# K partial sums seeded into PSUM, adaLN spans of 1024 columns and a token-major gate/up in one decoder block on one Trainium2 core

## The chip, the cores and the metric

The kernel runs on one NeuronCore of a Trainium2 chip. The core has five engines with a program each: TensorE (PE, matmuls into the accumulators in PSUM), VectorE (DVE), ScalarE (ACT), GpSimd (POOL) and SyncE (SP, which here issues nearly all DMA transfers). They wait for each other through semaphores, and each runs its own instructions in order. The metric is the device time of one execution in microseconds (us), taken as the median of the runs shown.

## What is computed

One decoder layer on 256 tokens with 2048 channels, in fp32. All projections are written as three matmuls in a rounded fp32 format: each operand is split into a high part and the rest, and high x high, high x rest and rest x high are summed in PSUM. Cut to what matters:

```python
mod = silu(c) @ ada_w + ada_b                    # 2048 x 12288
sh1, sc1, g1, sh2, sc2, g2 = split(mod, 6)       # adaLN, 2048 columns each
h = rms_norm(x, mix_pre_g) * (1 + sc1) + sh1
q, k, v, a, g = split(h @ w_in)                  # 2048 x 5120, 1024 columns each
attn = moba_attention(q, k, v)                   # 8 heads, 256 tokens are one key block: causal attention
u = causal_depthwise_conv(a * sigmoid(g), conv_w, conv_b)   # 1024 channels, 31 taps
u = silu(layer_norm(u, conv_ln_g, conv_ln_b))
x = x + g1 * rms_norm(concat(attn, u) @ w_out, mix_post_g)  # 2048 x 2048
h = rms_norm(x, ffn_pre_g) * (1 + sc2) + sh2
y = (silu(h @ w_gate) * (h @ w_up)) @ w_down     # 2048 x 5632 twice, 5632 x 2048
out = x + g2 * rms_norm(y, ffn_post_g)
```

## The kernel before

**Tiles.** The 256 tokens are two tiles of 128 (t = 0, 1; NT in the code). The K dimension is cut into blocks of 128 rows, output columns into groups of 512. A weight load brings up to four K blocks of one group, 1 MB, into one of five raw buffers (`weights`, L595; L619 and L636 are variants for short segments). ACT copies the high part of two K blocks into `wh` (L610), DVE subtracts it for the rest `wl` (L611), and TensorE multiplies.

**Jobs.** A `Job` (L289) is one output group over one segment of K. It holds two of the four PSUM tiles `pa`, one for each t. `multiply_all` (L656) cuts it into units of one or two K blocks and one t. There are two forms. In `mm` (L677) the tokens are the stationary operand and 512 weight columns move: three matmuls for a K block, the result lies token-major. In `side` (L668) 128 weight columns are stationary and all 256 tokens move: six matmuls of 256 columns for a K block and t (t then names one half of the output columns), and the result lies channel-major, as the next stage wants it. Before, `side` is used for all of w_in but v, and for gate and up; `mm` for v, w_out and w_down.

**Partial sums.** Where K is cut into segments, `put` (L709) stores the first segment's result from PSUM to SBUF on ACT (L715) and adds each later one to it on DVE (L717). The last segment is added in the same way; what follows (sigmoid and product for a and g, silu and product for gate and up, the square for the norm of y, L954) then reads SBUF. In w_in the cuts come from `cuts`: four segments for a and g (groups 6 to 9), three for groups 0, 2, 4 and four for groups 1, 3, 5 (the q, k, v columns). w_out has two segments, w_down three (`parts`), gate and up of the first four FFN groups four each (`fcuts`); the other seven FFN groups run over all of K.

**adaLN.** `ada` (L453) makes one span of 512 (or, in early chunks, 256) columns of one of the six vectors from loads of 1 MB (96 in all). Each load is summed on PE (L476: the vector c, padded to 32 columns, against the load; four K blocks in four strips of the array at once) or on DVE (L485, L487: multiply by a column of c and add to a tile `t2`). The letter in `mode` decides: p is PE, d is DVE, a is open: the planner gives each load to PE, but leaves it to DVE when DVE has nothing queued. `sums` (L518) then sums over the partitions for shift and scale columns, L512 spreads the gate rows g1 and g2 over all partitions, and L514 multiplies them into `gain`. There are three tiles in the `t2` pool; adaLN sums, attention, the chunks of h and the gate products share them.

**Stages.** `chunks` cuts K of w_in: for each chunk the spans of SC1 and SH1 are made, then that chunk of h (`h_chunk`, L534), then the w_in segments that end there. When all of a and g is there, `conv` (L759) runs: `nact` of eight channel tiles are multiplied by the taps on ACT (L788) and added on DVE (L791), the others run on DVE alone (L774). `layer_norm` (L804) and then the second K half of w_out wait for it. `attention` (L873) runs in between. Then come y1's norm, x1, `h2_chunk` (L1113), gate and up (`gate_evac` L978, `up_evac` L994), w_down in three parts, and the last norm with the output stores (L1186, L1187).

**Order.** The program is written by a planner (`Plan.order`, L154). It simulates the engines with a cost for each task and emits the tasks in the order in which they start there, so each engine's order is fixed at build time. On each engine the ready task with the smallest `pri` goes first; matmul units of the projections have 3.0, evacuations 0.0. DMA loads come from two queues, weights and adaLN. An adaLN load goes ahead of the weights from weight index `before`, may use a gap from index `after`, and otherwise weights go first while fewer than `nw` are open. For G1 these are `g1_before` and `g1_from`, for SC2 and SH2 `c_before` and `c_after`.

Of the kernel before, what the change touches and what calls it, by code (L numbers as in the profile page):

```python
# [16 lines left out]
P = 128  # L17
D = 2048
# [25 lines left out]
 'g1_before': 23,  # L44
 'c_before': (-192, -5, 77, 198),
 'first': 0,
 'pri': {'conv': 10.889,
         'att': 1.269,
         'g1': 2.484,
         's2': 2.504,  # L50
         'g2': 8.462,
         'cap': 1.455,
         'ln': 2.276,
         'glu': 6.517,
         'h': 0.32,
         'turn': 7.06,
         'hid': 8.565,
         'h2': 2.033},
 'silu': 1,
 'h1': 'DADDDADA',  # L60
 'h2': 'DADDAAAA',
# [4 lines left out]
 'nact': 6,  # L66
 'stagger': 4,
 'stagger1': 4,
 'joint': 2,
# [7 lines left out]
 'g1_from': 51,  # L77
 'c_after': (50, 119, -180, -13),
 'g2_from': 0}
# [209 lines left out]
class Job:  # L289
# [11 lines left out]
def block_kernel(ctx, tc, x, c, ada_w, ada_b, mix_pre_g, mix_post_g, w_in, conv_w, conv_b,  # L301
# [16 lines left out]
    hd_pool = ac_pool = t2_pool  # L318
    if CFG["uni"] < 2:
        hd_pool = Slots([sbt([P, 512], "hd%d" % i) for i in range(CFG["heads"])])  # L320
    if CFG["uni"] < 1:
        ac_pool = Slots([sbt([P, 512], "ac%d" % i) for i in range(CFG["acc"])])
    pri = CFG["pri"]
    br_pool = Slots([sbt([1, 512], "brow")])
# [14 lines left out]
        "w0": ("Q0", [P, 2, 2, 512], F32R), "w1": ("Q1", [P, 2, 2, 512], F32R), "w2": ("Q2", [P, 2, 2, 512], F32R),  # L339
        "conv": ("CV", [P, CT * (256 + HALO) + CT * 256], F32), "x1": ("CV", [P, NT, D], F32),  # L340
# [44 lines left out]
    nc.vector.memset(mhalf, -0.5)  # L385
    cpad = sbt([P, KB, 32], "cpad")
# [835 lines left out]
```

## Time and profile before

| what | value |
|---|---|
| median of 3 runs | 1223.05 us (1222.06 to 1223.63) |
| the profiled execution's own time | 1223.58 us |
| its span, first to last instruction | 1221.8 us |
| mean granted TensorE clock | 0.993 |
| DMA | 307.71 MB, mean 252 GB/s |
| adaLN loads | 96 of 1 MB, median 7.4 us from issue to landing |
| POOL busy | 16.2 us |

In a row of the profile, PE is TensorE's matmuls and PEld its weight loads, which overlap them. L717 is line 717 of the kernel before. The records of a matmul are longer than the distance between two of them, since they are pipelined: the pace is read from the starts, not from the lengths. In the page's slices each digit is the busy share of a fortieth of the span in tenths.

### The profile page before, as it was taken

The numbers are of one execution on the slowest core, as the hardware profiler recorded it, in microseconds if no ns is written. First come the engines' busy times: TensorE is split into PE (matmuls) and PEld (weight loads), VectorE is DVE, ScalarE is ACT, GpSimd is POOL, SyncE is SP. The second block draws the span as 40 slices with busy tenths as digits, with TensorE's granted clock in tenths as the row PEclk, the third lists the DMA queues.
The fourth block names the chain that finished last, engine by engine and source line by source line (L and its number), as shares of the span: only waits on it lengthen the run. The fifth ranks groups of instructions, "written<-read, shape, count | busy, mean of one in ns | idle before, by whom it ended". The sixth has DMA issues, their size and how long they took to land.

```text
span 1221.8 us, 19898 instructions
## 1 busy us (share of the span) xinstructions
PE 1196.4 (98%) x8275; PEld 1072.2 (88%) x8275; DVE 877.6 (72%) x1121; ACT 599.7 (49%) x860; POOL 16.2 (1%) x29
## 2 busy tenths in 40 slices
PE   5999999999999989999999999999999999999997
PEld 4899799997558769999998789999988999999886
DVE  4799889999978789998788996444555455455554
ACT  3643344998965465534454344434433444444441
POOL 1000000000000010000000000000000000000000
PEclk9999999999998999999999999999999999999999
DMA  9999996558997989988558997655556555555532
GB/s 334 343 341 340 370 348 207 177 179 302 343 383 253 326 315 375 323 297 274 173 185 324 365 363 254 196 174 179 198 175 192 187 173 184 195 173 179 200 104 69
DMA packets 160507, 307.71 MB, mean 252 GB/s; under 512 B 5244, under 2 KB 21920, under 8 KB 159648
## 3 DMA queue, kind: packets, MB, share of 16 engines
q1 hardware_dynamic: 159520, 304.11, 72.5%
q0 software_dynamic: 544, 2.11, 0.5%
q8 instruction: 65, 1.06, 0.4%
q10 hardware_dynamic: 352, 0.21, 0.1%
q14 instruction: 26, 0.21, 0.0%
HBM read 304.32 MB, written 2.10 MB: 251 GB/s over the span
## 4 chain that ended last, share of the span: by engine, by line
PE 89%; ACT 4%; DMA 3%; DVE 1%; issue 1%; SPq 1%; POOL 0%; POOLq 0%; DVEq 0%; ACTq 0%
PE pa L674 54%; PE pa L680 10%; PE pa L682 10%; PE pa L681 10%; PE pt L476 3%; DMA raw<-in_ada_w_dram 2%; ACT prod L788 2%; ACT wh L610 1%; PE pt L518 1%; DMA xt<-in_x_dram 1%; DVE t L487 1%; PE pt L512 1%; SPq L626 0%; DVE wl L611 0%; PE pt L825 0%
## 5 line engine op out<-in xcount | busy, mean ns | idle before, releaser
L674 PE MATMUL pa<-h,wh 128*128 128x256 f32 x3840 | 701.6, 284 | 0.0
L611 DVE TENSOR_TENSOR wl<-raw,wh 128x1024 fp32r<-128x1024 f32 x372 | 451.3, 1223 | 271.8 <-ACT wh L610 270.8
L610 ACT ACTIVATE wh<-raw 128x1024 fp32r<-128x1024 f32 x372 | 392.6, 1060 | 498.0 <-PE pa L674 291.1
L674 PEld LDWEIGHTS pa<-h,wh 128*128 128x128 f32 x3840 | 593.9, 188 | 6.4 <-issue 2.7
L674 PE MATMUL pa<-h,wl 128*128 128x256 f32 x1920 | 540.9, 282 | 0.0
L674 PEld LDWEIGHTS pa<-h,wl 128*128 128x128 f32 x1920 | 363.9, 190 | 0.5 <-issue 0.2
L487 DVE SCALAR_TENSOR_TENSOR t<-raw,cact,t 128x512 f32<-128x512 f32 (+1 forms) x238 | 160.9, 676 | 7.6 <-DVE stats L832 0.3
L680 PE MATMUL pa<-wh,hid 128*128 128x512 f32 x352 | 140.9, 400 | 0.0
L682 PE MATMUL pa<-wh,hid 128*128 128x512 f32 x352 | 139.6, 397 | 0.0
L681 PE MATMUL pa<-wl,hid 128*128 128x512 f32 x352 | 139.6, 397 | 0.0
L681 PEld LDWEIGHTS pa<-wl,hid 128*128 128x128 f32 x352 | 66.4, 189 | 16.5 <-issue 0.7
L680 PEld LDWEIGHTS pa<-wh,hid 128*128 128x128 f32 x352 | 66.4, 189 | 16.5 <-issue 0.7
L682 PEld LDWEIGHTS pa<-wh,hid 128*128 128x128 f32 x352 | 66.4, 189 | 16.1
L788 ACT ACTIVATE prod<-conv,taps 128x256 f32<-128x256 f32 x180 | 74.9, 504 | 0.2 <-DVE conv L791 0.2
L791 DVE TENSOR_TENSOR conv<-conv,prod 128x1536 f32<-128x1536 f32 x30 | 52.6, 1753 | 2.1 <-ACT prod L788 1.9
L476 PE MATMUL pt<-raw,cpad 128*32 128x512 f32 (+1 forms) x384 | 45.7, 571 | 5.5 <-DMA raw<-in_ada_w_dram 5.4
L476 PEld LDWEIGHTS pt<-raw,cpad 128*32 128x32 f32 x384 | 9.1, 114 | 21.7 <-issue 10.0
L680 PE MATMUL pa<-wh,mixa 128*128 128x512 f32 x64 | 28.0, 438 | 0.0
L680 PE MATMUL pa<-wh,h 128*128 128x512 f32 x64 | 26.9, 421 | 0.0
L682 PE MATMUL pa<-wh,mixa 128*128 128x512 f32 x64 | 26.3, 412 | 0.0
L681 PE MATMUL pa<-wl,mixa 128*128 128x512 f32 x64 | 26.3, 410 | 0.0
L774 DVE SCALAR_TENSOR_TENSOR conv<-conv,taps 128x256 f32<-128x256 f32 x60 | 25.7, 480 | 0.0
(154 smaller groups left out, 786.5 us busy)
## 6 DMA issues: line engine op xcount, KB each, us to landing
raw<-in_ada_w_dram SPq DMA_DIRECT2D x96, 1024.0 KB, 7.4
raw<-in_w_gate_dram SPq DMA_DIRECT2D x44, 1024.0 KB, 5.3
raw<-in_w_up_dram SPq DMA_DIRECT2D x44, 1024.0 KB, 5.2
raw<-in_w_down_dram SPq DMA_DIRECT2D x44, 1024.0 KB, 5.1
raw<-in_w_in_dram SPq DMA_DIRECT2D x32, 1024.0 KB, 6.8
raw<-in_w_out_dram SPq DMA_DIRECT2D x16, 1024.0 KB, 7.9
raw<-in_w_in_dram SPq DMA_DIRECT2D x16, 512.0 KB, 7.4
xt<-in_x_dram SPq DMA_DIRECT2D x2, 1024.0 KB, 10.1
```

The source lines that it names most:

```text
L476: nc.tensor.matmul(ps.t[32 * (k % 4):32 * (k % 4) + 32, 0:wd], cpad[:, k0 + k, :], view()[:, k, :], start=me == mine[0] and k < 4, stop=me ...
L487: nc.vector.scalar_tensor_tensor(acc.t[:, 0:wd], view()[:, k, :], s, acc.t[:, 0:wd], op0=ALU.mult, op1=ALU.add)
L512: a = add("PE", 0.86, min(prio, pri["cap"]), lambda: nc.tensor.matmul(pt.t, ones, acc.t, start=True, stop=True), [a], [pt, acc])
L610: a = add("ACT", 0.475 * m, p, lambda raw=raw, u=u, m=m, wh=wh: nc.scalar.activation(wh.t[:, 0:m, :], raw.t[:, u:u + m, :], AF.Copy), [loa ...
L611: b = add("DVE", 0.567 * m, p, lambda raw=raw, u=u, m=m, wh=wh, wl=wl: nc.vector.tensor_sub(wl.t[:, 0:m, :], raw.t[:, u:u + m, :], f32(wh. ...
L674: nc.tensor.matmul(job.ps[t].t[:, 256 * n:256 * n + 256], w.t[:, j, cs], h, start=u == 0 and j == r and n == 0 and i == 0, stop=end and j ...
L680: nc.tensor.matmul(job.ps[t].t, hi, wh.t[:, j, :], start=u == 0 and j == r, stop=False)
L681: nc.tensor.matmul(job.ps[t].t, hi, wl.t[:, j, :], start=False, stop=False)
L682: nc.tensor.matmul(job.ps[t].t, lo, wh.t[:, j, :], start=False, stop=end and j == r + len(ks) - 1)
L774: nc.vector.scalar_tensor_tensor(cacc[:, k, :], upad[:, k, i:i + 256], w, cacc[:, k, :], op0=ALU.mult, op1=ALU.add)
L788: nc.scalar.activation(T("prod")[:, i % 2, k, :], upad[:, k, i:i + 256], AF.Copy, scale=w)
L791: pa = add("DVE", 0.267 * CFG["nact"] + 0.07, pri["conv"] + 0.001 * i, lambda i=i: nc.vector.tensor_add(cacc[:, nv:], cacc[:, nv:], T("pro ...
```

## The change

1. **Seeds (`inj`).** A job whose group has an earlier segment gets a `base`: before its first matmul ACT copies the stored partial sum from SBUF into the job's PSUM tile, and all its matmuls accumulate onto it. The copy waits for the earlier segment's store and until the job before it has issued its first unit. The result of every segment but the last is copied out on ACT; the last one is read from PSUM where it is used. The DVE adds of `put` are gone.
2. **adaLN spans.** `ada` takes any span of K columns; of 1024 columns it keeps two sums (two tiles, or on PE two rows of strips in one PSUM tile). G1 and SC2/SH2 are cut 512, 512, 1024, G2 1024, 1024; the chunks of w_in lose the cut at 6. The modes change: in loads, 28 p, 20 a and 48 d become 12 p, 48 a and 36 d.
3. **Token-major gate/up.** Gate and up use `mm`. The product of silu(gate) and up lies token-major, is turned by four PE transposes for each group and t, and is split into high part and rest from PSUM.
4. **Order.** New priorities, cuts, loading order of adaLN, conv channels on ACT (`nact` 6 to 5), and split of the tiles at the ends of w_out and w_down (`stagger`, `stagger1`, `joint`). In `side` the two matmuls with `wh` now follow each other. The output stores alternate between SP's and ACT's queues.

The core of the diff:

```diff
- 'g1_before': 23,
- 'c_before': (-192, -5, 77, 198),
+ 'g1_before': 68,
+ 'c_before': (-94, -6, 151, 326),
...
- 'pri': {'conv': 10.889, 'att': 1.269, 'g1': 2.484, 's2': 2.504, 'g2': 8.462, 'cap': 1.455, ...
-         'turn': 7.06, 'hid': 8.565, 'h2': 2.033},
+ 'pri': {'conv': 5.107, 'att': 2.483, 'g1': 2.378, 's2': 1.948, 'g2': 8.002, 'cap': 2.527, ...
+         'hid': 0.937, 'h2': 0.789, 'base': 0, 'turn': 1.308},
- 'nact': 6, 'stagger': 4, 'stagger1': 4, 'joint': 2,
+ 'nact': 5, 'stagger': 7, 'stagger1': 6, 'joint': 1,
- 'mode': {1: 'pdap', 0: 'daad', 2: 'papp', 4: 'padd', 3: 'dpdd', 5: 'dddd'},
- 'chunks': (0, 2, 4, 6, 8, 12, 16),
- 'cuts': ((0, 2, 6, 12, 16), (0, 2, 6, 16), (0, 4, 6, 8, 16)),
+ 'mode': {1: 'paaa', 0: 'dada', 2: 'dpad', 4: 'aaad', 3: 'pada', 5: 'dada'},
+ 'chunks': (0, 2, 4, 8, 12, 16),
+ 'cuts': ((0, 2, 8, 12, 16), (0, 2, 4, 8, 12, 16), (0, 4, 16)),
- 'g1_from': 51, 'c_after': (50, 119, -180, -13), 'g2_from': 0}
+ 'g1_from': 27, 'c_after': (-49, 104, -34, 37), 'g2_from': 0,
+ 's2': ((0, 4), (4, 8), (8, 16)), 'g1': ((0, 4), (4, 8), (8, 16)), 'g2': ((0, 8), (8, 16)),
+ 'inj': 1}
...
 def multiply_all(pairs, stagger):
+        for i, (units, job) in enumerate(pairs):
+            if job.base is not None and CFG["inj"]:
+                for t in range(NT):
+                    place, deps = job.base(t)
+                    last[i][t] = add("ACT", 0.48, pri["base"], lambda ...: nc.scalar.activation(job.ps[t].t, place(), AF.Copy),
+                                     deps + begun[-1], [job.ps[t]])
+            begun.append([])
...
-                        for i, (w, h) in enumerate(((wh, hi), (wl, hi), (wh, lo))):
+                        for i, (w, h) in enumerate(((wh, hi), (wh, lo), (wl, hi))):
...
-    def put(dst, job, last, first, prio=0.0, more=()):
-            if first:
-                ts.append(add("ACT", ..., nc.scalar.activation(dst(t), job.ps[t].t, AF.Copy), ...))
-            else:
-                ts.append(add("DVE", ..., nc.vector.tensor_add(dst(t), dst(t), job.ps[t].t), ...))
+    def put(dst, job, last, prio=0.0, more=()):
+        return [add("ACT", ..., nc.scalar.activation(dst(t), job.ps[t].t, AF.Copy), ...) for t in range(NT)]
+    def base_of(place, made, key):
+        if key not in made:
+            return None
+        tasks = made[key]
+        return lambda t: (lambda: place(t), [tasks[t]])
...
 def up_evac(g, slot):
+                a = add("DVE", 0.69, 0.0, ... nc.vector.tensor_mul(z.t, z.t, job.ps[t].t), [last[t], ga], [job.ps[t], z])
+                pt = Buf(pt_pool)
+                def turn(z=z, pt=pt):
+                    for k in range(4):
+                        nc.tensor.transpose(pt.t[:, P * k:P * k + P], z.t[:, P * k:P * k + P], ident)
+                a = add("PE", 0.434, pri["turn"], turn, [a], [z, pt])
...
-                weights(w, 0, 512 * g, list(range(k0, k1)), Job(pa_pool, h2_stat, h2_deps, ev, True))
+                weights(w, 0, 512 * g, list(range(k0, k1)), Job(pa_pool, h2_stat, h2_deps, ev, base=part_base(i)))
...
-        for groups, cuts in (((6, 8, 7, 9), CFG["cuts"][0]), ...
+        for groups, cuts in (((8, 6, 9, 7), CFG["cuts"][0]), ...
...
-                nc.sync.dma_start(out[P * t:P * t + P, sl], T("x1")[:, t, sl])
+                (nc.scalar if i % 2 else nc.sync).dma_start(out[P * t:P * t + P, sl], T("x1")[:, t, sl])
```

More of the change, by code (lines that the diff above doesn't have):

```diff
@@ L462, in ada, with all_pe @@
         parts = []
+        def all_pe():
+            return all(x.eng == "PE" for x in parts)
         for k0 in range(0, KB, per):
@@ L502, in choose @@
             def choose(t):
                 if any(x.eng == "DVE" for x in parts):
-                    t.eng, t.cost = "DVE", 0.63 if any(x.eng == "PE" for x in parts) else 0.0
-            prev = add("ACT", 0.48, prio, store, [prev], [ps, acc])
+                    t.eng, t.cost = "DVE", 0.63 * nc2 if any(x.eng == "PE" for x in parts) else 0.0
+            prev = add("ACT", 0.48, prio, store, [prev], [ps] + acc)
             prev.late = choose
-        pt = Buf(pt_pool)
         if m in (G1, G2):
@@ L516, in sums @@
-        def sums():
-            for j in range(n):
-                nc.tensor.matmul(pt.t[:, j:j + 1], acc.t[:, P * j:P * j + P], ones[:, 0:1], start=True, stop=True)
-        a = add("PE", 0.72, min(prio, pri["cap"]), sums, [prev], [pt, acc])
+            pts = [Buf(pt_pool) for _ in range(nc2)]
+            o = m * D + P * c0
+            a = plan.fetch(prio, lambda: nc.gpsimd.dma_start(br.t[0:64 * nc2 - 63:64, :], ada_b[:, o:o + P * n].rearrange("o (h n) -> (o h) n", n=512)), [prev], 0.01, [br])
@@ new lines, in ada @@
+            a = add("DVE", 0.602 * nc2, prio, bias, [a], [br] + acc)
+            a = add("PE", 0.86 * nc2, min(prio, pri["cap"]), spread, [a], pts + acc)
+            ends = []
+            for h in range(nc2):
+                g = gain[:, P * c0 + 512 * h:P * c0 + 512 * h + 512]
+                ends.append(add("DVE", 0.602, prio, lambda g=g, h=h: nc.vector.tensor_mul(g, g, pts[h].t), [a] + list(deps0), [pts[h]]))
+            return ends
+        pt = Buf(pt_pool)
+        def sums():
+            for j in range(min(n, 4)):
+                if all_pe() and nc2 == 2:
+                    nc.tensor.matmul(pt.t[:, 2 * j:2 * j + 2], acc[0].t[:, P * j:P * j + P], sel, start=True, stop=True)
+                else:
+                    for h in range(nc2):
+                        nc.tensor.matmul(pt.t[:, nc2 * j + h:nc2 * j + h + 1], acc[h].t[:, P * j:P * j + P], ones[:, 0:1], start=True, stop=True)
@@ L690, in multiply_all @@
         for i, (_, job) in enumerate(pairs):
+            if job.base is not None and not CFG["inj"]:
+                for t in range(NT):
+                    place, deps = job.base(t)
+                    last[i][t] = add("DVE", 0.602, 0.0, lambda job=job, t=t, place=place: nc.vector.tensor_add(job.ps[t].t, place(), job.ps[t].t),
+                                     deps + [last[i][t]], [job.ps[t]])
             job.evac(job, last[i])
@@ L1010, in f @@
+                l = add("DVE", 0.602, pri["hid"], lambda pt=pt, part=part: nc.vector.tensor_sub(part(1), pt.t.rearrange("p (k n) -> p k n", k=4), f32(part(0))), [h], [pt])
                 HID[slot][t] = [h, l]
+                PARTD.append(last[t])
         return f
     def project(kind, j, k0, k1):
-        return Job(pa_pool, h_stat, h1_deps, (ag_evac if kind >= 3 else qkv_evac)(kind % 3, j, k0 == 0, k1 == KB), kind != 2)
+        evac, place, made = (ag_evac, ag_place, AGD) if kind >= 3 else (qkv_evac, qkv_place, QKV)
```

296 lines of the change are left out of this document (157 added, 139 removed).

## The prediction, made before the changed kernel ran

> **What bounds the kernel now.** I read the page first: span and busy times, the slices of PE and DVE, and the shares of the chain that ended last.
>
> ```profile
> span 1221.8 us, 19898 instructions
> ...
> PE 1196.4 (98%) x8275; PEld 1072.2 (88%) x8275; DVE 877.6 (72%) x1121; ACT 599.7 (49%) x860; POOL 16.2 (1%) x29
> ...
> PE   5999999999999989999999999999999999999997
> ...
> DVE  4799889999978789998788996444555455455554
> ...
> PE 89%; ACT 4%; DMA 3%; DVE 1%; issue 1%; SPq 1%; POOL 0%; POOLq 0%; DVEq 0%; ACTq 0%
> ```
>
> TensorE ends the kernel: 89% of the chain, and it is full in nearly every slice. VectorE is full only in the first 60%. A busy PE is not proof of PE at its pace, so next I read the stages.
>
> ```profile
> 0.00:50.00 50.00, 37.48 (x290) 31.42 (x291) 25.22 (x56) 20.20 (x29) 4.37 (x13) 0.93 1.00 340
> 50.00:200.00 150.00, 149.90 (x1182) 136.91 (x1181) 135.81 (x202) 65.55 (x80) 0.00 (x0) 1.00 0.97 338
> ...
> 400.00:450.00 50.00, 45.63 (x245) 31.80 (x244) 38.14 (x60) 26.33 (x50) 5.24 (x5) 1.00 0.91 326
> 450.00:750.00 300.00, 300.00 (x2121) 280.60 (x2120) 261.96 (x324) 137.37 (x164) 1.46 (x3) 1.00 0.85 298
> ```
>
> ```profile
> 213.00:358.00 145.00, 143.85 (x907) 111.97 (x905) 140.61 (x198) 136.89 (x300) 1.46 (x3) 1.00 0.77 271
> ```
>
> The columns are PE, PE's weight loads, DVE, ACT and POOL busy, then the clock, the DMA share and GB/s. TensorE loses time at the start (12.5 us idle by the record, waiting for the first loads), 4.4 us in 400 to 450, between w_out and gate/up, and at the end. From 450 it loses nothing, in the slices of the page up to the last. The row that stands alone is the conv stage, from the first conv product on ACT to the last: DVE 140.6 and ACT 136.9 of 145 us. LayerNorm waits for it, and the second half of w_out for LayerNorm. So there are two limits: TensorE's own work after LayerNorm, and before it the time at which conv ends.
>
> **The change part by part.**
>
> **1. Pace of gate/up.** Pieces of the chain (start, length, what; L476, L681 and the start of gate/up at 449.1 serve parts 4 and 6), then the first and the last of 15 starts of one line in w_down, one for each set of three matmuls:
>
> ```profile
> 146.14 0.87 PE pt L555 x8
> ...
> 317.76 0.99 PE pt L476 x8
> ...
> 449.10 1.54 PE pa L674 x12
> ...
> 938.27 184.32 PE pa L674 x1536
> ```
>
> ```profile
> 433.97 0.24 PE pa L681
> ```
>
> ```profile
> 1178.65 0.40 PE L680 MATMUL pa<-wh,hid 128*128 128x512 f32 x1
> ...
> 1188.49 0.39 PE L680 MATMUL pa<-wh,hid 128*128 128x512 f32 x1
> ```
>
> Gate/up now issues six matmuls of 256 columns for a K block and an output half; 184.32 / 1536 = 0.120 us each, so 0.720. Token-major issues three of 512, as w_down does: (1188.49 - 1178.65) / 14 = 0.703 for three. There are 11 groups x 2 matrices x 16 K blocks x 2 = 704 such sets: 704 x 0.017 = **-12.0 us**, all on the path.
>
> **2. Its price.** The hidden product must now be turned: 11 x 2 x 4 = 88 transposes. Eight of L555 took 0.87 us, 0.109 each: **+9.6 us** on TensorE, also on the path. Their copies (ACT high part, DVE rest) stay as many as now.
>
> ```profile
> L1119 PE MATMUL pt<-ident,t x32: 270/273/328, 438.4 to 510.5; 128*128 128x128 f32 x32
> ```
>
> The Trainium skill, "TensorE: Matmul & The Clock Gate", Part 4: PE-mode transpose, speaks against this: it gives some 275 ns for a 128x128 transpose in a kernel; by that the price would be 88 x 0.275 = 24.2 us and gate/up would lose 12. The trace has 273 ns as the length of one (row above), but starts lie 109 ns apart, so I hold to the pace and keep the length as a rival.
>
> **3. Adds become seeds.**
>
> ```profile
> L717 DVE TENSOR_TENSOR part<-part,pa x36: 678/681/689, 502.7 to 628.4; 128x512 f32<-128x512 f32 x36
> L717 DVE TENSOR_TENSOR qkv<-qkv,pa x30: 680/683/692, 111.0 to 303.3; 128x512 f32<-128x512 f32 x30
> L717 DVE TENSOR_TENSOR ag<-ag,pa x24: 680/683/690, 86.1 to 210.5; 128x512 f32<-128x512 f32 x24
> L717 DVE TENSOR_TENSOR y<-y,pa x24: 679/681/690, 395.7 to 1212.6; 128x512 f32<-128x512 f32 x24
> L717 DVE TENSOR_TENSOR gain<-gain,pa x12: 679/682/689, 539.0 to 639.9; 128x512 f32<-128x512 f32 x12
> L954 ACT ACTIVATE pa<-y x16: 580/584/603, 397.3 to 1213.3; 128x512 f32<-128x512 f32 x16
> ```
>
> DVE loses 126 adds of 0.68, 86 us. ACT gains 126 seeds (nearest row L954, which also goes from SBUF to PSUM: 0.59) and 86 further copies out (52 first copies now, 126 + 12 then): 212 x 0.59 = 125 us, on 600 busy of 1222. After 450 neither costs anything while ACT is at most half full (137 of 300; were it full, each 1 us more would end 1 us later). What a seed can cost is a wait of TensorE: it may start only when the job before it has issued its first unit. A four-block job lasts 5.6 us (8 sets of 0.70) and its first unit 2.8, which leaves 2.8 us for two seeds of 0.59 and at worst one weight piece of 1.06 (L610, below) ahead of them on ACT: no wait. Two-block jobs (three of them, groups 0, 2, 4) leave nothing: some 1 us each. What queues behind a waiting seed on ACT is the next weight piece, whose DVE half and matmuls follow. Bounds: 0, and 126 / 2 jobs x 0.6 = 38 if every job waited for one seed; I take **+1**, near 0, because the slack is counted.
>
> **4. adaLN.** 41 of 96 loads run on PE now (8 records to a load of 512 columns, 16 to one of 256: 272/8 + 112/16), 0.99 us each (chain row). The modes now fix 28 on PE and 48 on DVE and leave 20 open; then 12, 36 and 48. An open load goes to DVE where DVE has nothing queued. Bounds: 12 or 60 on PE, -29 to +19 us of PE work. The groups by form; then three single rows of the view by stage: the adds L717 in 50 to 200, the same in the conv stage, and L487, the adaLN sums on DVE, in the conv stage (none):
>
> ```profile
> L611 DVE TENSOR_TENSOR wl<-raw,wh 128x1024 fp32r<-128x1024 f32 x372 | 451.3, 1223 | 271.8 <-ACT wh L610 270.8
> L610 ACT ACTIVATE wh<-raw 128x1024 fp32r<-128x1024 f32 x372 | 392.6, 1060 | 498.0 <-PE pa L674 291.1 <-PE pa L682 122.6 <-DMA raw<-in_w_in_dram 26.7
> ...
> L487 DVE SCALAR_TENSOR_TENSOR t<-raw,cact,t 128x512 f32<-128x512 f32 x171 | 128.4, 751 | 5.2 <-DVE stats L832 0.3
> L788 ACT ACTIVATE prod<-conv,taps 128x256 f32<-128x256 f32 x180 | 74.9, 504 | 0.2 <-DVE conv L791 0.2
> ...
> L791 DVE TENSOR_TENSOR conv<-conv,prod 128x1536 f32<-128x1536 f32 x30 | 52.6, 1753 | 2.1 <-ACT prod L788 1.9
> L476 PE MATMUL pt<-raw,cpad 128*32 128x512 f32 x272 | 35.6, 604 | 4.3 <-DMA raw<-in_ada_w_dram 4.2
> ...
> L774 DVE SCALAR_TENSOR_TENSOR conv<-conv,taps 128x256 f32<-128x256 f32 x60 | 25.7, 480 | 0.0
> ...
> L476 PE MATMUL pt<-raw,cpad 128*32 128x256 f32 x112 | 10.1, 491 | 1.2 <-DMA raw<-in_ada_w_dram 1.2
> ```
>
> ```profile
> 50.00:200.00 150.00, 25.14 (x38) 1.00 0.97 338
> ```
>
> ```profile
> 213.00:358.00 145.00, 8.22 (x12) 1.00 0.77 271
> ```
>
> ```profile
> 213.00:358.00 145.00, 0.00 (x0) 1.00 0.77 271
> ```
>
> On DVE a load of 512 columns costs four L487: 3.0 us. In 50 to 200 DVE has 14 us free now and drops 25 us of adds, room for 13 loads; I take five off PE, since an open load goes there only when nothing is queued: -5 us before conv. After 450 DVE is freed too (the 48 gate/up adds are gone), so open loads there go to DVE and cost nothing; were that cover missing, the eight of SC2's last span would cost 8 us.
>
> **5. When conv ends.** The a and g columns are complete after 112 K blocks of w_in instead of 106 (the new cuts): 6 x 12 x 0.120 = +8.6, with part 4's -5 it is +3.6. Then the stage itself: ACT hands one of six channels to DVE, 30 x 0.50 = -15, gets 12 seeds and 12 copies (the last segments of q, k and v), +14, and three weight pieces of 1.06 fewer (48 K blocks are left after a and g, not 54, two to a piece): about -4. DVE gets 30 x 0.48 = +14, a sixth of L791 less = -9, its 12 adds less = -8, three L611 less = -4: -7. The fuller engine, DVE, falls from 140.6 to 134. +3.6 - 7 = **-3**. TensorE has 1.2 us idle in that stage and 5 us less to do before it, so it can follow. The bounds: -9 (all open loads off PE) and +14 (second rival).
>
> **6. From w_out to gate/up.**
>
> ```profile
> 427.66 0.69 DVE L717 TENSOR_TENSOR y<-y,pa 128x512 f32<-128x512 f32 x1 [2.12 <-PE pa L682]
> 435.28 0.68 DVE L717 TENSOR_TENSOR y<-y,pa 128x512 f32<-128x512 f32 x1
> 444.12 0.69 DVE L1142 TENSOR_TENSOR h<-t,h 128x512 fp32r<-128x512 f32 x1
> 447.72 0.69 DVE L1142 TENSOR_TENSOR h<-t,h 128x512 fp32r<-128x512 f32 x1
> ```
>
> w_out's last set begins its second matmul at 433.97, so it ends at about 434.4, and gate/up begins at 449.1: 14.7 us, because a matmul of 256 columns needs both token tiles. Token-major needs one. From a tile's add to its h2 took 17.2 (tile 0) or 13.1 (tile 1); without the add, 16.5 or 12.4; tile 0 will end 2.8 us before w_out does. First matmul 9.6 to 13.7 us after w_out: gain 1.0 to 5.1, I take **-3**. G1's loads, allowed from weight index 27 and not 51, use the DMA hole of the conv stage (share 0.77 there); that is cover for the S2 loads, not a term.
>
> **7. End.** The last add goes, 0.69; output stores alternate on ACT's queue, whose issue lies beside SP's:
>
> ```profile
> 1212.58 0.69 DVE L717 TENSOR_TENSOR y<-y,pa 128x512 f32<-128x512 f32 x1 [0.19 <-PE pa L682]
> ```
>
> **-0.7**. The 1024-column spans' single store and sums save under 2 us where all is on PE; taken as 0, hidden by conv. The new order of a K block's six matmuls in w_in, the larger row buffer, the scratch outputs of the squares and the later tile split of w_out's tail change no count on the path: 0. Each wide span holds two of three t2 tiles, which can hold back attention; that belongs to the second rival.
>
> Sum: -12.0 + 9.6 + 1 - 3 - 3 - 0.7 = **-8.1**. The profiled execution took 1223.58 us, 1.8 more than its span: 1215.5. The median is 0.5 below that execution: **1215**.
>
> **Rivals.** *DVE relief is used in full*: open loads leave PE before conv (10 instead of 5: -5) and at 400 to 450 (-3), and the gap closes by 5, not 3: 1215 - 10 = 1205. For: DVE is what is full in 50 to 350. Against: with conv pending, DVE has work queued, and open loads then stay on PE. *Conv ends later (slower)*: G1's first span changes from PE to DVE, four loads of 3.0 = 12 us. In the conv stage DVE runs no adaLN at all now, so if these fall there, DVE's 134 becomes 146, 5 over today; with the a and g columns 8.6 later and no relief, conv ends 13.6 later instead of 3 earlier: 1215 + 16.6 = 1232. It decides from the point where conv's end slips by more than 5.1 us, the sum of my other terms. For: DVE and ACT are both over 94% busy there. *Nothing but the pace*: parts 5 and 6 give 0 and seeds cost 2: -12.0 + 9.6 + 2 - 0.7 = -1.1, 1222. *Transposes take their length*: 88 x (0.273 - 0.109) = 14.4 more: 1229. *The seeds don't work as meant* would change results, not times; it has no price here.
>
> **Chances.** Forecast 0.40, relief in full 0.20, only pace 0.15, conv later 0.20, transposes 0.05. The first two are faster: 0.60; the third is the same: 0.15; the last two slower: 0.25. A measurement of this kernel tells 0.2%, 2.4 us, from no change. The range takes in 1205 and 1229 with the further bounds of part 4 and the slip of conv in part: 1200 to 1231; the forecast's own is 1210 to 1220.
>
> **What would show it.** Right: 0.703 us for three gate/up matmuls; transposes 0.11 apart; no adds L717; ACT near 710 us busy, DVE near 800; PE busy without gaps after the first gate/up matmul, which comes near 443 us; the last conv product near 350. Wrong: gaps before seeded jobs in which PE waits for ACT; L487 work inside the conv stage with LayerNorm after 385; more than 45 adaLN loads on PE after LayerNorm or in the FFN.

## The result, and the profile after

The changed kernel took **1202.01 us** (median of 4 runs, 1200.84 to 1203.41), the kernel before 1223.34 beside it (1222.06 to 1223.89): a ratio of 0.9828, 95% interval 0.9811 to 0.9845. That is 21 us faster; the forecast was 8. The sign was right and the time lies in the range, but near its low end, so most of the gain isn't in the sum. Line numbers below are those of the changed kernel (L739 to L741 are the three matmuls of `mm`, L733 is `side`, L718 a seed, L857 a conv product on ACT, L1083 a transpose, L505 an adaLN sum on DVE).

The page of the kernel after: span and busy times, the slices of PE, DVE and ACT, the chain that ended last.

```profile
span 1200.6 us, 15816 instructions
...
PE 1179.0 (98%) x6191; PEld 967.5 (81%) x6191; DVE 812.5 (68%) x1024; ACT 693.3 (58%) x1039; POOL 10.8 (1%) x26
...
PE   6999999999999999999999999999999999999997
...
DVE  4689889899997798964569984554444454445453
ACT  3566767898996575787664444444444444444441
...
PE 93%; DMA 3%; ACT 2%; issue 1%; DVE 1%; SPq 1%; POOL 0%; DVEq 0%; POOLq 0%; ACTq 0%
```

DVE and ACT stand where the prediction had them (800 and 710 busy; 812.5 and 693.3 measured), and TensorE bounds the kernel more than before (93% of the chain for 89%). The view by stage, columns as in the prediction:

```profile
50.00:200.00 150.00, 149.56 (x1161) 139.88 (x1160) 131.32 (x171) 104.11 (x155) 0.00 (x0) 1.00 1.00 363
223.00:358.00 135.00, 133.37 (x845) 103.48 (x844) 130.80 (x215) 126.98 (x278) 0.55 (x1) 1.00 0.77 277
...
450.00:750.00 300.00, 300.00 (x1329) 242.61 (x1322) 217.59 (x254) 176.92 (x240) 0.55 (x1) 1.00 0.81 290
```

The conv stage (second row) is still full on DVE and ACT, and TensorE loses nothing in the FFN, now as before. So a gain can only come from TensorE's own work and from the gaps. Most of it lies early: the first gate/up matmul starts at 431.0 for 449.1 before, so 18 of the 21 us are won ahead of it and 3 behind it.

The rows of 350 to 400, before and after, show one difference that isn't work:

```profile
350.00:400.00 50.00, 50.00 (x240) 37.25 (x239) 39.92 (x56) 25.55 (x41) 1.84 (x3) 0.93 0.85 303
```

```profile
350.00:400.00 50.00, 49.97 (x235) 41.25 (x234) 36.83 (x47) 32.78 (x54) 1.84 (x3) 1.00 0.61 211
```

TensorE is full in both, but the granted clock is 0.93 in the trace before and 1.00 in that after. By an estimate from these rows, 0.07 x 50 = 3.5 us of the 21 in these two traces are the clock's. In e13 below, whose plan is nearly that of after, the same row has 0.97, so this part isn't shown to belong to the change.

The next fence has two rows of the timeline in the last w_down job, 21 matmuls apart:

```profile
1186.49 0.39 PE L741 MATMUL pa<-wh,hid 128*128 128x512 f32 x1
...
1191.37 0.39 PE L741 MATMUL pa<-wh,hid 128*128 128x512 f32 x1
```

(1191.37 - 1186.49) / 7 = 0.697 us for three matmuls. The same loop took 0.703 before (the prediction's w_down rows), and **the change doesn't touch the form of w_down**. The prediction had named 0.703 as the pace to see. This was the lead: something had made these matmuls faster by about 1%.

What differs for w_down is where its tiles lie. By the program's allocation of SBUF, the weight tiles `wh` and `wl` begin at a multiple of 128 bytes in both kernels. The activation tiles (h, mixa, mixc, hid) lie behind a row of small tiles, at 96 beyond a multiple of 128 before. The change puts one small tile more in front of them, `sel` of two columns, which takes 32 bytes and moves them all to a multiple of 128. My theory for the experiments was that this place sets the pace; the rivals were that any change of the program shifts it, or that the rest of the gain comes from the lighter DVE.

### The profile page after: what moved, and what is told of

It is laid out like the page before. It is cut to its first block, busy times and chain, and to the rows that moved or that the text cites. A ratio compares the mean times of both kernels' runs of the same rounds, so it can differ in the third digit from the quotient of the medians.

```text
span 1200.6 us, 15816 instructions
## 1 busy us (share of the span) xinstructions
PE 1179.0 (98%) x6191; PEld 967.5 (81%) x6191; DVE 812.5 (68%) x1024; ACT 693.3 (58%) x1039; POOL 10.8 (1%) x26
## 4 chain that ended last, share of the span: by engine, by line
PE 93%; DMA 3%; ACT 2%; issue 1%; DVE 1%; SPq 1%; POOL 0%; DVEq 0%; POOLq 0%; ACTq 0%
PE pa L739 24%; PE pa L741 24%; PE pa L740 24%; PE pa L733 14%; PE pt L492 2%; DMA raw<-in_ada_w_dram 2%; DMA xt<-in_x_dram 1%; PE pt L560 1%; PE pt L1083 1%; SPq L675 0%; PE pt L544 0%; ACT prod L857 0%; ACT wh L659 0%; PE pt L880 0%; ACT qkv L777 0%
## 5 line engine op out<-in xcount | busy, mean ns | idle before, releaser
L739 PE MATMUL pa<-wh,h 128*128 128x512 f32 x768 | 305.6, 398 | 0.5 <-DVE h L1219 0.5
L741 PE MATMUL pa<-wh,h 128*128 128x512 f32 x768 | 303.2, 395 | 0.0
L740 PE MATMUL pa<-wl,h 128*128 128x512 f32 x768 | 303.1, 395 | 0.0
L733 PE MATMUL pa<-h,wh 128*128 128x256 f32 x1024 | 189.2, 287 | 1.5 <-DVE h L628 1.1
L739 PEld LDWEIGHTS pa<-wh,h 128*128 128x128 f32 x768 | 144.5, 188 | 37.6 <-issue 4.2
L741 PEld LDWEIGHTS pa<-wh,h 128*128 128x128 f32 x768 | 144.5, 188 | 34.5 <-DVE h L1220 0.4
L740 PEld LDWEIGHTS pa<-wl,h 128*128 128x128 f32 x768 | 144.6, 188 | 32.9
L733 PEld LDWEIGHTS pa<-h,wh 128*128 128x128 f32 x1024 | 158.7, 190 | 13.0 <-issue 8.0
L505 DVE SCALAR_TENSOR_TENSOR t<-raw,cact,t 128x512 f32<-128x512 f32 (+1 forms) x238 | 163.4, 715 | 4.1 <-DMA raw<-in_ada_w_dram 0.2
L733 PE MATMUL pa<-h,wl 128*128 128x256 f32 x512 | 144.7, 283 | 0.0
L739 PE MATMUL pa<-wh,hid 128*128 128x512 f32 x352 | 140.0, 398 | 0.0
L741 PE MATMUL pa<-wh,hid 128*128 128x512 f32 x352 | 138.9, 395 | 0.0
L733 PEld LDWEIGHTS pa<-h,wl 128*128 128x128 f32 x512 | 97.1, 190 | 0.0
L739 PEld LDWEIGHTS pa<-wh,hid 128*128 128x128 f32 x352 | 66.3, 188 | 15.8 <-ACT wh L659 0.2
L741 PEld LDWEIGHTS pa<-wh,hid 128*128 128x128 f32 x352 | 66.3, 188 | 15.7
L857 ACT ACTIVATE prod<-conv,taps 128x256 f32<-128x256 f32 x150 | 63.0, 507 | 4.8 <-DVE conv L860 4.8
L860 DVE TENSOR_TENSOR conv<-conv,prod 128x1280 f32<-128x1280 f32 x30 | 44.5, 1484 | 0.9 <-ACT prod L857 0.5
L492 PE MATMUL pt<-raw,cpad 128*32 128x512 f32 (+1 forms) x320 | 40.3, 597 | 2.3 <-DMA raw<-in_ada_w_dram 2.3
```

Source lines behind the costliest of these rows:

```text
L492: nc.tensor.matmul(ps.t[o:o + 32, 0:wd], cpad[:, k0 + k, :], view()[:, k, wd * h:wd * h + wd], start=me == mine[0] and k < strips, stop=me ...
L505: nc.vector.scalar_tensor_tensor(acc[h].t[:, 0:wd], w, s, acc[h].t[:, 0:wd], op0=ALU.mult, op1=ALU.add)
L733: nc.tensor.matmul(job.ps[t].t[:, 256 * n:256 * n + 256], w.t[:, j, cs], h, start=(job.base is None or not CFG["inj"]) and u == 0 and j == ...
L739: nc.tensor.matmul(job.ps[t].t, hi, wh.t[:, j, :], start=(job.base is None or not CFG["inj"]) and u == 0 and j == r, stop=False, skip_grou ...
L740: nc.tensor.matmul(job.ps[t].t, hi, wl.t[:, j, :], start=False, stop=False, skip_group_check=job.base is not None and bool(CFG["inj"]))
L741: nc.tensor.matmul(job.ps[t].t, lo, wh.t[:, j, :], start=False, stop=end and j == r + len(ks) - 1, skip_group_check=job.base is not None a ...
```

## The experiments

The last column is the ratio times 1223 us, less 1223.

| run | median us | ratio to before, 95% | us against before |
|---|---|---|---|
| after | 1202.01 | 0.9828 (0.9811 to 0.9845) | -21.0 |
| e1_before_shift32 | 1212.38 | 0.9908 (0.9876 to 0.9939) | -11.3 |
| e2_after_shift32 | 1204.98 | 0.9846 (0.9811 to 0.9881) | -18.8 |
| e3_after_dve_adds | 1237.87 | 1.0123 (1.0108 to 1.0138) | +15.0 |
| e4_after_side | 1211.61 | 0.9895 (0.9866 to 0.9924) | -12.8 |
| e5_after_both | 1209.81 | 0.9887 (0.9849 to 0.9924) | -13.8 |
| e6_before_noshift | 1223.27 | 1.0004 (0.9990 to 1.0017) | +0.5 |
| e7_before_shift64 | 1211.62 | 0.9921 (0.9894 to 0.9948) | -9.7 |
| e8_before_shift96 | 1195.87 | 0.9781 (0.9761 to 0.9802) | -26.8 |
| e9_after_shift64 | 1187.36 | 0.9705 (0.9688 to 0.9723) | -36.1 |
| e10_after_old_plan | 1273.50 | 1.0397 (1.0371 to 1.0424) | +48.6 |
| e11_after_narrow | 1221.12 | 0.9987 (0.9972 to 1.0002) | -1.6 |
| e12_before_front | 1223.56 | 0.9999 (0.9981 to 1.0017) | -0.1 |
| e13_after_narrow_modes | 1204.76 | 0.9850 (0.9826 to 0.9875) | -18.3 |
| e14_after_nact6 | 1209.25 | 0.9892 (0.9871 to 0.9914) | -13.2 |

### The place of the activation tiles

**e1, e6, e7, e8, e12: the kernel before, nothing changed but addresses.** e1, e7 and e8 put one tile behind `mhalf`, of 32, 64 and 96 bytes (2, 16 and 24 columns; the first rounds up to 32 bytes):

```diff
     nc.vector.memset(mhalf, -0.5)
+    shift = sbt([P, 2], "shift")
+    nc.vector.memset(shift, 0.0)
```

> The kernel before, with nothing changed but a tile of two columns (32 bytes a partition, cleared once) laid where the change lays its selector tile. Every tile behind it, h, the hidden product, the mixer's output and the partial sums among them, moves by 32 bytes. Theory A (pace by address): the matmuls of before are slower because these tiles lie 32 bytes off a multiple of 64; here the 256-column matmul falls from 0.1200 to about 0.1186 us and the 512-column one from 0.2343 to about 0.2324, and the time falls by 5760 x 0.0014 + 1632 x 0.0019 = 11 us, to about 1212. Rival B (the shorter pace after the change comes from how it accumulates or what runs beside it): paces and time as before, 1222 to 1224.

> The kernel before with 64 bytes in front of the tiles behind mhalf, in place of the 32 of e1_before_shift32. Theory A (tiles that begin at a multiple of 64 bytes run at 232.4 ns, others slower): the tiles lie at 32 beyond a multiple of 64, so slow or between, 1218 to 1225 us with 233.3 or 234.3 ns. Theory B (any shift or any change gives the faster pace): about 1212 us with 232.4 ns.

> The kernel before with 96 bytes in front of the tiles behind mhalf. Theory A: the tiles lie at a multiple of 64 bytes again, 232.4 and 118.65 ns, about 1212 us as e1_before_shift32. Theory C (only a multiple of 128 bytes helps): 234.3 or 233.3 ns, 1218 to 1225 us.

e6 has the same extra instruction, on columns that fit into the 32 bytes `mhalf` has anyway, so nothing moves:

```diff
-    mhalf = sbt([P, 2], "mhalf")
+    mhalf = sbt([P, 4], "mhalf")
...
+    nc.vector.memset(mhalf[:, 2:4], 0.0)
```

> The kernel before, with the same extra memset as in e1_before_shift32 (a few elements of one tile), but with the elements taken within the 32 bytes that mhalf has anyway, so that no tile behind it moves. Theory A (the place of the tiles in SBUF sets the pace): nothing changes, 1222 to 1226 us, 512-column pitch 234.3 ns and 256-column pitch 120.0 ns as in the kernel before. Theory B (any change of the program, one instruction more, shifts the pace): about 1212 us with 232.4 and 118.65 ns, as e1_before_shift32.

e12 puts 96 bytes ahead of all tiles. The activation tiles then lie exactly where e8 has them, but the weight tiles have moved along:

```diff
+    front = sbt([P, 24], "front")
     raw_pool = Slots([sbt([P, 4, 512], "raw%d" % i) for i in range(CFG["raw"])], Plan.REUSE)
```

> The kernel before with 96 bytes in front of all tiles, weights included, so that the tiles behind mhalf lie where e8_before_shift96 has them (64 beyond a multiple of 128 bytes), but weight tiles and activation tiles keep the distance that they have in the kernel before. Theory A (the distance between the weight tile and the activation tile counts): 1221 to 1226 us with 234.3 and 120.0 ns. Theory B (the address of the activation tiles alone counts): 1193 to 1198 us with some 229 ns. Theory C (any tile off a multiple of 64 bytes costs): 1226 us or more.

Pieces of the chain (start, length, what): the same 1536 gate/up matmuls of 256 columns in the last FFN stretch, in e6, e12, e1, e7 and e8 in this order. In the kernel before this piece is 184.32 long (a row of the prediction).

```profile
937.44 184.32 PE pa L675 x1536
```

```profile
938.38 184.32 PE pa L676 x1536
```

```profile
929.09 182.27 PE pa L676 x1536
```

```profile
745.94 123.89 PE pa L676 x1044
...
937.01 180.22 PE pa L676 x1536
```

```profile
731.76 122.96 PE pa L676 x1044
...
921.92 174.10 PE pa L676 x1536
```

No clock, no wait and no instruction differs in these pieces, only their length: 0.1200 us a matmul in before, e6 and e12, 0.1187 in e1, 0.1173 in e7, 0.1133 in e8. e6 rules out that any edit does it: with the instruction added and nothing moved, 1223.27 us. e12 rules out that the place of the activation tiles alone counts: they lie as in e8, but the weight tiles moved with them, and the piece is as long as in before to the last digit, the time the same within 0.2%. What e1, e7 and e8 change and e12 doesn't is the **distance between weight tile and activation tile**. (The distance of every other tile behind `mhalf`, the partial sums among them, to the tiles in front changes with it; the two that a matmul reads are the likely pair, but no run moves them alone.)

My theories of *which* distances are good fell. e7 was expected slow by "a multiple of 64 bytes" and took 1211.6; e8 was expected at 1212 and took 1195.9, 16 us less than either theory had. The distances are counted modulo 128 bytes here; no run tells 128 from a longer period. By the runs, activation tiles at 96 bytes beyond the weight tiles are slowest, at 0 and 32 some 10 us faster, and at 64 some 27 us faster.

**e2, e9: the same in the kernel after.** e2 adds 32 bytes (32 modulo 128), e9 adds 64:

```diff
     nc.vector.memset(mhalf, -0.5)
+    shift = sbt([P, 16], "shift")
+    nc.vector.memset(shift[:, 0:2], 0.0)
```

> The changed kernel with one more such tile of 32 bytes, which takes the tiles behind it off the multiple of 64 again. Theory A: 256-column matmuls back to 0.1200, 512-column ones to 0.2343, time up by 1536 x 0.0014 + 3744 x 0.0019 = 9 us, to about 1211. Rival B: as the changed kernel, 1201 to 1203.

> The kernel after with 64 bytes in front of the tiles behind mhalf, so that they begin at 64 beyond a multiple of 128 bytes, as in e8_before_shift96 (after has them at 0, as e1_before_shift32). Theory A (the place sets the pace of the matmuls in this kernel too): 512-column pitch near 229 ns in place of 232.4 and a time of 1183 to 1190 us, as much below the kernel after as e8_before_shift96 (1195.9) was below e1_before_shift32 (1212.4). Theory B (the kernel after has another bound, or the pace belongs to the kernel before alone): 1199 to 1204 us.

The transposes of a group serve as marks: from one set of eight to the next lie one set and the 192 matmuls of 512 columns of a group's gate and up. The chain of after, e2 and e9:

```profile
1011.89 0.88 PE pt L1083 x8
1057.38 0.87 PE pt L1083 x8
1103.05 0.87 PE pt L1083 x8
```

```profile
1012.56 0.87 PE pt L1085 x8
1058.24 0.87 PE pt L1085 x8
```

```profile
1002.25 0.87 PE pt L1085 x8
1047.09 0.87 PE pt L1085 x8
```

Less 0.87 and divided by 192: 0.2324 us in after (0.2333 in its next group, to 1103.05), 0.2334 in e2, 0.2290 in e9. So e9 met theory A. Its step from after (15.1 us) is that from e1 to e8 (15.5 us), which have the same two places: the place is a term by itself, and adds to the rest of the change. e9, at **1187.36 us**, is the fastest kernel of this study, 36 us below before. e2 met neither theory: its pace is slower than after's in the first of these groups, as A had it, but by 1.0 ns and not 1.9, and equals after's in the next; the time is longer only by 2 us, within the intervals.

### Token-major gate/up

**e4: the kernel after with channel-major gate/up as before** (`side`, six matmuls of 256 columns; no transposes, and high part and rest are taken from the product in SBUF as before).

```diff
-                weights(..., Job(pa_pool, h2_stat, h2_deps, ev, base=part_base(i)))
+                weights(..., Job(pa_pool, h2_stat, h2_deps, ev, True, base=part_base(i)))
```

> The changed kernel with gate and up channel-major as before (six matmuls of 256 columns, both token tiles needed, no transposes), all else as changed. Theory A: from the first gate/up matmul to the last matmul of w_down the time changes little, 704 x (0.712 - 0.697) - 9.6 = +0.7 us at the paces of the changed kernel, and what token-major brought lies before it: the first gate/up matmul comes 4 to 9 us later than 431. Total 1206 to 1212. Rival (token-major is worth much in the FFN itself): the FFN is longer by over 5 us. Rival (token-major brings nothing anywhere): 1201 to 1204.

**e5: token-major, but every unit waits for both token tiles of h2**, so that only the early start is taken away.

```diff
-        return H2[kb // 4][t]
+        return H2[kb // 4][0] + H2[kb // 4][1]
```

> The changed kernel, token-major, but each gate/up unit waits for the h of both token tiles, as the channel-major form did. Theory A (the gap between w_out and gate/up closed because one tile is enough): the first gate/up matmul comes 4 to 9 us later, the FFN behind it is unchanged, total 1206 to 1211. Rival (it closed because the adds are gone or the adaLN loads come earlier): 1201 to 1204.

The timeline around the first gate/up matmul: w_out's last matmul and gate/up's first, in e4, in e5, and in after (there also ACT's squares of w_out's last group for the two token tiles, L1030):

```profile
424.69 0.40 PE L741 MATMUL pa<-wh,mixc 128*128 128x512 f32 x1
436.85 0.36 PE L733 MATMUL pa<-h,wh 128*128 128x256 f32 x1
```

```profile
428.02 0.40 PE L741 MATMUL pa<-wh,mixc 128*128 128x512 f32 x1
440.20 0.48 PE L739 MATMUL pa<-wh,h 128*128 128x512 f32 x1
```

```profile
420.33 0.60 ACT L1030 ACTIVATE junk<-pa 128x512 f32<-128x512 f32 x1 [1.80 <-PE pa L741]
...
425.73 0.60 ACT L1030 ACTIVATE junk<-pa 128x512 f32<-128x512 f32 x1 [0.35 <-PE pa L741]
```

```profile
425.24 0.40 PE L741 MATMUL pa<-wh,mixc 128*128 128x512 f32 x1
...
431.00 0.50 PE L739 MATMUL pa<-wh,h 128*128 128x512 f32 x1 [0.46 <-DVE h L1219]
```

From the start of w_out's last matmul to gate/up's first lie 12.2 us in e4 and in e5, and 5.8 in after. So the early start is worth 6.4 us in the gap, and e5's whole time agrees (7.2 us above after). The gap is short because tile 0 leaves w_out 5.4 us ahead of tile 1 (425.73 - 420.33), and its way to the first matmul is then 10.7 us. All of token-major is worth 8.2 us by e4's ratio, 9.6 by the medians, in the range of e4's theory A, but not by its working. From the first gate/up matmul to w_down's last, e4 takes 763.8 us (436.85 to 1200.60) and after 760.4 (431.00 to 1191.37): 3.4 more where the theory had 0.7. Two of e4's pieces, of 1152 and 1536 matmuls, ran at 0.1200 us and not at e1's 0.1187, which makes 3.6 us (the longer one stands under "Still open" below). So 6 of the 8 to 10 us are the early start; the rest is of the size of this pace, and not shown to be token-major's.

### The plan: seeds, conv stage, adaLN

**e3: the partial sums added on VectorE again, no seeds.** Nothing else differs.

```diff
- 'inj': 1}
+ 'inj': 0}
```

> The kernel after with the partial K sums added on VectorE in PSUM as before, no seeds by ScalarE; all else as in the kernel after. Theory A (the seeds are free for TensorE and the lighter VectorE is worth some us in idle time between stages): 1204 to 1210 us, VectorE some 60 us busier and ScalarE less busy by the seeds. Rival (the seeds hold TensorE's first matmul of a job back, as the prediction's part 3 had as its bound): faster than the kernel after, 1190 to 1200 us. No part of it: within 1200 to 1204 us.

The stage 50 to 200 and the conv products of e3, then the conv products of after:

```profile
50.00:200.00 150.00, 142.66 (x1074) 130.18 (x1073) 140.32 (x192) 73.10 (x99) 0.00 (x0) 0.95 0.98 351
```

```profile
L857 ACT ACTIVATE prod<-conv,taps x150: 491/498/533, 245.8 to 381.7; 128x256 f32<-128x256 f32 x150
```

```profile
L857 ACT ACTIVATE prod<-conv,taps x150: 490/502/564, 223.7 to 354.3; 128x256 f32<-128x256 f32 x150
```

36 us slower than after, far past theory A's bound. DVE goes from 131 to 140 busy of 150 us ahead of conv, TensorE loses 7 us there, at a granted clock of 0.95 in place of 1.00, and takes 19 adaLN loads ahead of conv and not 11; conv starts 22 us and ends 27 us later. The new plan gives DVE work that it has room for only without the adds. What the seeds themselves cost TensorE is small. The view of L718 in after, who waited for it (us, times):

```profile
who waited for it (us, times):
  ACT wh L659: 1.5, 2
  PEld pa L733: 1.5, 2
  PE pa L733: 0.4, 1
```

**e11: adaLN spans of 512 columns for G1, S2 and G2.** The modes were left as in after, so G1's last 512 columns got the fourth letter, d, which the wide span doesn't use: four loads more of G1 are fixed on DVE. (The last letters of SC2/SH2 and of G2 count in e11 too.) **e13** gives both halves of each wide span its engine.

```diff
- 's2': ((0, 4), (4, 8), (8, 16)), 'g1': ((0, 4), (4, 8), (8, 16)), 'g2': ((0, 8), (8, 16)),
+ 's2': ((0, 4), (4, 8), (8, 12), (12, 16)), 'g1': ((0, 4), (4, 8), (8, 12), (12, 16)), 'g2': ((0, 4), (4, 8), (8, 12), (12, 16)),
- 'c_before': (-94, -6, 151, 326),
+ 'c_before': (-94, -6, 151, 151),
- 'c_after': (-49, 104, -34, 37),
+ 'c_after': (-49, 104, -34, -34),
```

and in e13 besides:

```diff
- 'mode': {1: 'paaa', 0: 'dada', 2: 'dpad', 4: 'aaad', 3: 'pada', 5: 'dada'},
+ 'mode': {1: 'paaa', 0: 'dada', 2: 'dpaa', 4: 'aaaa', 3: 'padd', 5: 'dddd'},
```

> The kernel after with the adaLN spans of G1, S2 and G2 of 512 columns, as before, and all else as in the kernel after (the two halves of a former wide span keep its place in the order). Theory A (the wide spans are worth nothing, as in the prediction): 1199 to 1205 us. Theory B (the wide spans spare stores, sums and waits on TensorE's path): 1206 to 1215 us. Theory C (wide spans hold two of three t2 buffers and hold attention back): 1190 to 1198 us.

> As e11_after_narrow (adaLN spans of G1, S2 and G2 of 512 columns), but both halves of a former wide span have the engine that the wide span has in the kernel after, so that G1's last four loads are no longer fixed on VectorE. Theory A (e11 was slow by those four loads in the conv stage alone, the width is worth nothing): 1199 to 1206 us, LayerNorm near 358 us as in the kernel after. Theory B (the width itself saves): 1208 to 1220 us.

e11's adaLN sums on DVE between 215 and 375, a group that after doesn't have there, with its conv products and its stage 350 to 375; then that stage in after, and e13's conv products:

```profile
L505 DVE SCALAR_TENSOR_TENSOR t<-raw,cact,t 128x512 f32<-128x512 f32 x15 | 11.3, 750 | 0.4
```

```profile
L857 ACT ACTIVATE prod<-conv,taps x150: 490/497/558, 222.7 to 373.1; 128x256 f32<-128x256 f32 x150
```

```profile
350.00:375.00 25.00, 18.88 (x95) 15.76 (x94) 25.00 (x35) 21.33 (x42) 0.00 (x0) 0.91 0.56 188
```

```profile
350.00:375.00 25.00, 24.97 (x128) 20.95 (x127) 19.28 (x26) 15.27 (x27) 0.72 (x1) 1.00 0.52 169
```

```profile
L857 ACT ACTIVATE prod<-conv,taps x150: 492/502/547, 221.4 to 351.1; 128x256 f32<-128x256 f32 x150
```

Four loads on DVE in the conv stage move conv's end to 373, from 351 in e13 (354 in after), and the time by 17 us (e11 against e13); TensorE runs out of work after 350. The other letters act later: e11 is 19 us behind e13 at LayerNorm's first matmul (374.4 for 355.2), and still 15 at gate/up's first (444.7 for 429.4). The width of the spans is worth nothing that shows: e13's interval overlaps that of after, as its theory A had it.

**e14: six conv channels on ScalarE, as before.**

```diff
- 'nact': 5,
+ 'nact': 6,
```

> The kernel after with six conv channels on ScalarE, as before, in place of five. ScalarE gets 30 products of 0.507 us more, 15 us, in a stage where it is busy 48 of 50 us; VectorE loses 30 of 0.477 and gains 30 x 0.27, 6 us less. Theory A (ScalarE with the seeds has no room in the conv stage, so the exchange is needed): conv ends 10 to 15 us later and the time is 1211 to 1217 us. Theory B (it has room, or other work moves out of the way): 1199 to 1205 us.

The conv products and the stage 300 to 350 of e14:

```profile
L857 ACT ACTIVATE prod<-conv,taps x180: 491/502/563, 223.2 to 361.2; 128x256 f32<-128x256 f32 x180
```

```profile
300.00:350.00 50.00, 47.12 (x245) 37.39 (x244) 44.42 (x58) 49.69 (x110) 0.00 (x0) 1.00 0.66 233
```

ACT is full (49.7 of 50), conv ends 6.9 us later and the time is 7.8 us longer. The direction is A's; the size lies between the two theories, presumably because other work of ACT moved behind the stage, which wasn't tried.

**e10: the code of after with the plan's numbers of before** (priorities, cuts, chunks, modes, `nact`, spans).

> The kernel after (seeds, token-major gate/up, the new order of six matmuls, tiles where after has them) with the plan's numbers of the kernel before: its order, its adaLN spans of 512 columns and their modes, six channels on ScalarE. Theory A (the new plan brings nothing of its own; the pace of the matmuls and token-major make the gain): 1199 to 1206 us, e1_before_shift32 (1212.4) less the 9.6 that token-major is worth. Theory B (seeds and plan belong together: with the old plan ScalarE is too full in the conv stage): 1207 to 1225 us. Theory C (the seeds alone relieve the conv stage and the new plan gives that back): 1188 to 1198 us.

49 us slower than before, past all three theories. Two places show in its profile: conv's products, and a hole of TensorE in the FFN (the view by stage, with DVE's largest group in that window).

```profile
L857 ACT ACTIVATE prod<-conv,taps x180: 490/500/565, 224.7 to 370.2; 128x256 f32<-128x256 f32 x180
```

```profile
690.00:712.00 22.00, 10.12 (x68) 8.71 (x67) 21.25 (x29) 0.70 (x2) 0.48 (x1) 0.78 0.96 328
```

```profile
L505 DVE SCALAR_TENSOR_TENSOR t<-raw,cact,t 128x512 f32<-128x512 f32 x23 | 17.3, 751 | 0.7
```

ACT with seeds and six channels ends conv at 370 (theory B), and G2's sums hold DVE, and with it the next weights, for some 20 us. The two don't make up all of the loss, and the run changes too much at once to say more than that the old numbers don't fit the new tasks.

## Why the prediction was right or wrong

**The step that failed** is the list in part 7, "change no count on the path: 0", and with it the sum's silent assumption that every matmul but those of gate/up keeps its pace. An edit was priced by the work that it issues. `sel` issues almost none, and wasn't even named; what it does is move all tiles behind it by 32 bytes. e1 measures that term alone, in the kernel before, at **-11.3 us** (interval -7.5 to -15.2), e6 and e12 are its controls. No run lays the kernel after at 96. With the paces measured at 96 and 0, its 1536 matmuls of 256 columns and 3744 of 512 give 1536 x 0.0013 + 3744 x 0.0019 = 9 us, an estimate; that e9 and e8 make the same step speaks for carrying the term over.

The forecast's -8.1 and -11.3 make -19.4; measured were -21.0. That they come so close is partly luck: with part 6 at its measured 9.2 in place of 3 the sum would be -25.6, and other terms, below, came out smaller than forecast.

**Part 1** (-12.0): the mechanism is right. At one place, 6 x 182.27 / 1536 = 0.712 us (e1) stand against 3 x 0.2324 = 0.697 (after): 704 x 0.015 = -10.6 us. In the FFN as a whole it can't be seen as a gain. From the first gate/up matmul to w_down's last, e1 takes 756.7 us (rows below), 3.7 less than after's 760.4, which holds 9.6 of transposes and two adaLN loads on TensorE; e4 takes 763.8. What parts 1 and 2 make together is open.

```profile
443.54 0.36 PE L676 MATMUL pa<-h,wh 128*128 128x256 f32 x1
...
1200.19 0.39 PE L684 MATMUL pa<-wh,hid 128*128 128x512 f32 x1
```

**Part 2** (+9.6): right to the digit; eight transposes take 0.87 us, so the 88 take 9.6. The rival in which they take their length of 273 ns is out: they follow each other at 109 ns. The Trainium skill, "TensorE: Matmul & The Clock Gate", Part 4: PE-mode transpose, gives some 275 ns for one in a kernel; that agrees with the length here and isn't the price.

**Part 3** (+1): right for what it priced; TensorE waited about 2 us in all for seeds (the rows of L718). What it left out is the other side. e3 shows that the new plan can't do without the seeds: 36 us. In the forecast the dropped adds were worth five loads less on PE and a part of conv's term. The freed room on DVE was filled anew, and so the plan has no place left for the adds.

**Part 4** (five loads fewer on PE, -5 before conv): right in the number, wrong in the place. The page's groups have 272 and 112 records of L476 before; in after L492 has 320, of which 256 are of 512 columns: 256/8 + 64/16 = 36 loads, 41 before. Ahead of conv (0 to 218 before, 0 to 223.7 after) the rows are:

```profile
L476 PE MATMUL pt<-raw,cpad x168: 378/592/637, 9.0 to 151.5; 128*32 128x256 f32 x112, 128*32 128x512 f32 x56
```

```profile
L492 PE MATMUL pt<-raw,cpad x120: 379/617/637, 9.1 to 220.7; 128*32 128x256 f32 x64, 128*32 128x512 f32 x56
```

That is 14 loads and 11: three fewer, not five. In the conv stage there are 16 and then 18, from there to gate/up 11 and 5, in the FFN none and 2.

**Part 5** (conv ends 3 earlier): wrong for the last product, which came at 354.3, before at 353.2:

```profile
L788 ACT ACTIVATE prod<-conv,taps x180: 489/498/546, 218.0 to 353.2; 128x256 f32<-128x256 f32 x180
```

Conv began later than forecast (223.7 for 218.0, so 5.7 and not 3.6; with three loads fewer the forecast's working gives 8.6 - 3 = 5.6) and the stage shrank by 4.6 and not 7 (from 135.2 to 130.6). What waits for conv was nevertheless earlier, and by most of the 3 us: LayerNorm's first matmul came at 358.1, before at 360.0. e14 shows that the exchange of a channel was needed, worth 7.8 us.

**Part 6** (-3, bounds 1.0 to 5.1): the mechanism is right (e5), the size is not. Counted as in the prediction, the gap went from 14.7 to 5.5, by 9.2 us. Of that 6.4 are the start with one tile; the other 2.8 e4 has as well, so they aren't token-major's. Two numbers were mis-sized: the lead of tile 0 at w_out's end, 2.8 us in the forecast and 5.4 in the trace, and tile 0's way to the first matmul, 12.4 to 16.5 in the forecast and 10.7 in the trace. The tile split of w_out's tail, another item of part 7's list at 0, is the setting that was changed there; it wasn't tried alone.

**Part 7** (-0.7 for the end): little seen. From the start of w_down's last matmul to the end of the span lie 9.2 us in after (1191.37 to 1200.6), 9.6 before (1212.15 to 1221.8).

**The rivals.** *Conv ends later* did not come about, since no adaLN sum of DVE falls into the conv stage. Its mechanism is right all the same: e11 puts four loads of G1 there, as the rival had it, and costs 17 us against e13. That the rival had 16.6 is luck: it took 5 us for these loads, the rest from other terms, and in e11 conv's end slips by 22 against e13. *Relief in full*, 1205, is nearest in time, but for another reason: 36 loads stayed on PE, and ahead of conv three left it, not ten. *Only the pace* had parts 5 and 6 at nothing; part 6 alone was 9.2 us.

Put together by ratios: place -11.3, token-major -8.2, and -1.5 for seeds, spans, order and ends together, which is the difference of e4 and e1 and lies within their intervals. Of the 8.2 only the early start is shown to be token-major's (6.4), and what the clock gave isn't separated in any of these terms. The large single terms (36 for the seeds, 8 for the channel, 17 for the place of four loads) are what the pieces of one plan are worth to each other, not gains over the plan before.

**Still open:** why the distance of tiles counts, and for which of the three products of a set, wasn't tried. Nor does the place alone fix the pace: the second piece of e4 below, with tiles at after's place, ran at 0.1200 us a matmul, where e1 had 0.1187, and e8's two pieces differ (122.96 / 1044 = 0.1178, then 0.1133). The order of the three products in `side`, which is another in e4 than in e1, isn't enough to explain it: e4's first piece below, in the same order as its second, still ran at 0.1187. What switches it within a run is not known.

```profile
516.70 112.50 PE pa L733 x948
...
927.45 184.32 PE pa L733 x1536
```

## What to carry to other kernels

When the same loop, untouched by the change, runs at another pace afterwards, look at where its tiles lie before looking for a cause in the order of the work: a small tile more or less in front of them can be worth as much as the rest of the change, and a run with that tile alone (and one that moves all tiles together) tells it. Before such a comparison, bring both kernels to the same distances; then try the few others, since one of them may be the cheapest gain to be had. And an edit that takes work off an engine is worth what the plan puts in its place: undo it alone in the new plan, and it may cost many times what it brought.

## What the runs showed that was not expected

The pace of these matmuls, each with its own weight load, changes with the distance between weight and activation tiles. At 96, 0, 32 and 64 bytes (modulo 128) in the kernel before the 256-column form took 120.0, 118.7, 117.3 and 113.3 ns in the last FFN stretch; the 512-column form took 234.3 at 96 (before, w_down), 232.4 at 0 (after), 233.4 at 32 (e2) and 229.0 at 64 (e9). The order isn't the same for both forms. Within one run, and at one distance, the pace can step from one such value to another (118.7 to 120.0 ns in e4, 232.4 to 233.3 in after), so the distance isn't all that sets it. The granted clock was full in all these stretches.
